# Loading the experts' weights as 16 KB per partition: a one-core transformer layer with expert choice

## Chip, core and metric

The kernel runs on one core of a Trainium2 chip, in one launch. The metric is device time in microseconds (us), the median of three runs. TensorE (PE) multiplies into PSUM, VectorE (DVE), ScalarE (ACT) and GpSimd (POOL) do the rest, and SyncE (SP) issues the loads, which 16 DMA engines carry from HBM to SBUF.

## What is computed

One encoder layer on x, 512 tokens of 1024 features, in float32. Three mixers (windowed attention, a short gated convolution, a bidirectional gated linear attention, GLA) work on one input projection, their outputs are merged by sigmoid gates, projected and added to the residual. Then comes the mixture of experts: 16 experts each choose their 64 best tokens.

```python
x = layer_norm(DN_ALPHA * x + merged @ w_out[l], ln_mix_g[l], ln_mix_b[l])
ffn = expert_choice_ffn(x, router_w[l], expert_w_gate[l], expert_w_up[l], expert_w_down[l])
x = layer_norm(DN_ALPHA * x + ffn, ln_ffn_g[l], ln_ffn_b[l])
# in expert_choice_ffn, for the 64 tokens xs of each expert:
h = jax.nn.silu(einsum('becd,edf->becf', xs, w_gate)) * einsum('becd,edf->becf', xs, w_up)
y = einsum('becf,efd->becd', h, w_down) * gate[..., None]
```

Each expert has three matrices of 8 MB (gate and up 1024 x 2048, down 2048 x 1024), 24 MB; all 16 have 403 million bytes. Everything else that is loaded is 43 million bytes.

## The kernel before

**Buffers.** Most of SBUF is one pool of 23 slots of 8 KB per partition (`S`, line 40). Every large tile of the whole program takes a slot and gives it back after its last reader. A load or a write into a slot that is not free waits for that reader.

**The front** (lines 75 to 755) splits the weights and x into high and low parts and computes the projections block by block; the GLA and attention steps are woven between the blocks. The loop of line 836 computes gates, branches and merge in 24 units, each with a load of 768 KB (`wmr`) that is split (`wmh`, `wml`). While it ends, the raw output weights (`wor`), the rows x (`xres`) and three loads of expert 0 are issued. The output projection runs as two passes (`pw`, `pw2`); the first adds to `xres` at line 924. In and behind the second pass lie the first norm and the router (lines 1032 to 1132): transposes of `xres` (`route_t`, line 938), the logits (`route_m`), the top tokens (`top64`), and the norm's scales and shifts spread over the partitions (`bcast`, line 1091).

**The experts** (lines 1287 to 1373) go in order e = 0 to 15, each gate (`g`), up (`u`) and down (`d`) in eight steps k. `gather` (line 1152) picks the tokens of a pair of experts with a one-hot matrix: in expert 0 for the first pair, in every odd expert for the next pair, one d-tile a step. `ff_mm` multiplies 64 tokens with 128 rows of the matrix, `down` with 256 rows; between them h is transposed (line 1368), and y is combined into the rows two experts later (`combine`). The last expert's down is done by blocks of 256 columns (`last_down`), then the second norm and the stores.

**The order of the loads** is the order of `seq` (line 798): one load of 1 MB per k. SP issues them in this order and stands at the first whose slot is not free.

```python
seq.append((eg[e, k * 128:(k + 1) * 128, :], e, "g", k))
seq.append((ed[e].rearrange("(h q p) d -> q p h d", h=2, p=128)[k], e, "d", k))
```

So a gate or up load brings each partition one row of 8 KB, a down load two rows of 4 KB, and a load of the last expert's down eight pieces of 1 KB. Three loads go out in the merge, 22 in all are queued behind the projection's first pass, 36 after the router, and the rest when the slots for `late`, `acc0` and `acc1` have been taken at the start of e0u (line 1317), where small POOL copies hold the order. Two spare buffers outside the pool take a load each (`early`, `hbt`).

Of the kernel before, what the change touches and what calls it, by code (L numbers as in the profile page):

```python
# [15 lines left out]
NE = 16  # L16
NSLOT = 23
# [4 lines left out]
HB, YB, NPRE, EARLY = 7, 15, 22, 3  # L22
# [6 lines left out]
def tile_hybrid_layer(ctx, tc, pk, w2p, xT, x, wlv, wa, wak, wmb, wout, eg, eu, ed, out):  # L29
# [4 lines left out]
    cpool = ctx.enter_context(tc.tile_pool(name="consts", bufs=1))  # L34
    spool = ctx.enter_context(tc.tile_pool(name="slots", bufs=NSLOT))
# [4 lines left out]
    def S(name, shape, dt=F32):  # L40
        n = 1
        for d in shape[1:]:
            n *= d
        assert n <= 2048
        t = spool.tile([128, 2048], dt, name=name, tag="s")
        v = t[:, :n]
# [4 lines left out]
        return v  # L51

# [22 lines left out]
    # ------------------------------------------------------------ first loads  # L75
    xr = [S(f"xr{i}", [128, 4, 512]) for i in range(2)]
    xh = [S(f"xh{i}", [128, 4, 512], F32R) for i in range(2)]
    xl = [S(f"xl{i}", [128, 4, 512], F32R) for i in range(2)]
    wr = [S(f"wlvr{i}", [128, 3, 672]) for i in range(3)]
    wh = [S(f"wlvh{i}", [128, 3, 672], F32R) for i in range(3)]  # L80
    wl = [S(f"wlvl{i}", [128, 3, 672], F32R) for i in range(3)]
# [9 lines left out]
    # the tensor engine's clock and the activation table are up before the first loads arrive  # L91
    v_sb = S("v_sb", [128, 4, 512])
# [13 lines left out]
    # ------------------------------------------------------------ constants  # L106
# [4 lines left out]
    at_t = S("at_t", [128, 2048])  # L111
# [20 lines left out]
    # ------------------------------------------------------------ GLA low rank, GLA v, attention v  # L132
    misc = S("misc", [128, 4, 512])          # low rank part, attention v, second key tile's decays
    av = misc[:, 1, :].rearrange("p (a b) -> p a b", a=4)
    # the low rank part is stacked three times on the partitions: high, low, high with high, high, low of its weights
# [8 lines left out]
    def b_mm(pb, k):  # L144
        """products of k-tile k, those first whose parts are there first"""
# [42 lines left out]
    raw = {}  # L188
    last_split = {}
# [4 lines left out]
    def load_unit(u, after):  # L194
        if u < 24:
            raw2[u] = S(f"wmr{u}", [128, 12, 128])
            load(raw2[u], wmb[u], after)

    def split_unit(u):
        if u >= 24:  # L200
            return
        h = S(f"wmh{u}", [128, 12, 128], F32R)
        l = S(f"wml{u}", [128, 12, 128], F32R)
        w2[u] = (h, l)
        A.copy(h, raw2[u])  # L205

        def low():
            sp2[u] = V.tensor_sub(l, raw2[u], f32(h))  # L208
            load_unit(u + 2, sp2[u])
        later.append(low)  # L210

    def load_chunk(c):
# [4 lines left out]
        raw[c] = S(f"wr{c}", [128, 2 if two else 1, 1024])  # L217
# [8 lines left out]
    def split_block(n, now=False):  # L226
# [4 lines left out]
        t = S(f"wb{n}", [128, 2, 1024], F32R)  # L231
# [28 lines left out]
    # ------------------------------------------------------------ GLA  # L260
    gqk = S("gqk", [128, 2, 2, 512])             # [q|k, tile, t]
    adec = {}                                    # (direction, tile) -> decay [128, 512]
# [48 lines left out]
    def ytile(b):  # L311
        y[b]["h"] = S(f"y{b}h", [128, 4, 512], F32R)
        y[b]["l"] = S(f"y{b}l", [128, 4, 512], F32R)
# [5 lines left out]

    class Gla:  # L320
        """one pass over the two heads of key tile i"""
# [8 lines left out]
        def start(self):  # L330
            i = self.i
            if i == 0:
                self.ps = S("gps0", [128, 4, 512])
# [3 lines left out]
            else:  # L337
                self.ps = S("gps1", [128, 2, 512])
# [5 lines left out]
        def prep(self, m):  # L344
            """factors of level m (blocks of 2m tokens, decays to the middle)"""
# [14 lines left out]
            if "qk2" not in st:  # L360
                st["qk2"] = S("qk2", [128, 2, 2, 512])
# [43 lines left out]
        def post(self, m):  # L405
            if m >= 256:
                # the rows of k and the state of each half of the tokens
# [8 lines left out]
            if m == 0:  # L416
                a = S(f"gA{self.i}", [128, 4, 512])
# [80 lines left out]
    def weave(a, b):  # L498
        """the steps of two lists in turn, so that neither waits for its own last step"""
# [7 lines left out]
    # ------------------------------------------------------------ attention  # L507
    aq = [S(f"aq{i}", [128, 4, 512], F32R) for i in range(2)]     # high and low parts
    ak = S("ak", [128, 2, 512], F32R)
# [9 lines left out]
    class Att:  # L519
        """heads j and j + 4, query block b"""  # L520
# [7 lines left out]
        def scores(self):  # L528
            j, b = self.j, self.b
            self.ps = [P("ps0"), P("ps1")]  # L530
            for g in range(2):
                hp = slice(g * 64, g * 64 + 64)
                for n, (lq, lk) in enumerate(((0, 0), (0, 1), (1, 0))):
                    PE.matmul(self.ps[g][:, :self.n], aq[lq][hp, j, b * 128:(b + 1) * 128],
                              ak[hp, lk, self.s0 * 128:self.s1 * 128], start=n == 0, stop=n == 2)
# [64 lines left out]
    # ------------------------------------------------------------ short convolution  # L600
# [25 lines left out]
    # ------------------------------------------------------------ side work beside the blocks  # L626
# [3 lines left out]
    class Step:  # L630
        """work beside a segment of the blocks: before it, on the tensor engine after it, and afterwards"""
# [38 lines left out]
    def overlay(a, b, at):  # L670
        """steps b beside steps a from position at of a"""
# [17 lines left out]
    def main_evac(nm, p):  # L689
# [5 lines left out]
        elif kind == "aq":  # L695
            h, l = (t[:, int(nm[2]), :] for t in aq)
            A.activation(h, p, AF.Copy, scale=0.125)
            later.append(lambda: V.scalar_tensor_tensor(l, p, 0.125, f32(h), op0=OP.mult, op1=OP.subtract))
        elif kind == "ak":
            A.copy(ak[:, 0, :], p)  # L700
            later.append(lambda: V.tensor_sub(ak[:, 1, :], p, f32(ak[:, 0, :])))
        elif kind == "gr":
            h = int(nm[2])
            if h == 0:
                st["rs"] = S("rsil", [128, 4, 512])
# [51 lines left out]
    # ------------------------------------------------------------ gates, branches, merge  # L757
    order = ("g", "c", "a")
    accs, mh, ml = [], [], []
    # ------------------------------------------------------------ output projection: its weights  # L760
# [6 lines left out]
    def load_wo(half, after):  # L767
        for c in range(2):
            wraw[half, c] = S(f"wor{half}{c}", [128, 4, 512])
# [3 lines left out]
    def load_rest(after):  # L773
        for i in range(2):
            xres.append(S(f"xres{i}", [128, 2, 1024]))
            load(xres[i], x[i * 256:(i + 1) * 256, :].rearrange("(a p) d -> p a d", p=128), after)
        load_wo(1, None)

    def wo_tiles(half, c):
        woh[half, c] = S(f"woh{half}{c}", [128, 4, 512], F32R)  # L780
        wol[half, c] = S(f"wol{half}{c}", [128, 4, 512], F32R)

    def wo_split(half, k):
        c = k // 4
        if (half, c) not in woh:
            wo_tiles(half, c)
# [10 lines left out]
    # ------------------------------------------------------------ expert weights  # L797
    seq = []
    for e in range(NE):
        for k in range(8):  # L800
            seq.append((eg[e, k * 128:(k + 1) * 128, :], e, "g", k))
        for k in range(8):
            seq.append((eu[e, k * 128:(k + 1) * 128, :], e, "u", k))
        for k in range(8):
            if e < NE - 1:
                seq.append((ed[e].rearrange("(h q p) d -> q p h d", h=2, p=128)[k], e, "d", k))
            else:
                src = ed[e].rearrange("(f p) d -> p f d", p=128)
                seq.append((src[:, k % 2 * 8:k % 2 * 8 + 8, k // 2 * 256:k // 2 * 256 + 256], e, "d", k))
    # the spare buffers take a load each: y's an early one, h's the last one before the experts begin  # L810
    seq = (seq[:EARLY] + [seq[YB]] + seq[EARLY:HB] + seq[HB + 1:YB] + seq[YB + 1:NPRE + 1] + [seq[HB]]
           + seq[NPRE + 1:])
    chunk = {}
    nload = [0]

    def load_experts(upto, after):
        while nload[0] < min(upto, len(seq)):
            src, e, kind, k = seq[nload[0]]
            if nload[0] == EARLY:
                t = st["spare"].tile([128, 2048], F32, name="early")  # L820
            elif nload[0] == NPRE:
                t = st["hbt"]
            else:
                t = S(f"e{e}{kind}{k}", [128, 2048])
            if kind == "d":
                t = t.rearrange("p (a b) -> p a b", a=src.shape[1])
            if nload[0] == len(seq) - 1:
                for f0, f1 in ((0, 4), (4, 6), (6, 8)):
                    load(t[:, f0:f1], src[:, f0:f1])
            else:  # L830
                load(t, src, after)
            after = None
            chunk[e, kind, k] = t
# [663 lines left out]
```

## Time and profile before

| what | value |
|---|---|
| three runs, device time | 1485.08, 1485.46, 1487.37 us (median 1485.46) |
| profiled execution: span of its core, its own time | 1485.3 us |
| mean granted TensorE clock | 0.989 |
| busy: PE, DVE, ACT, POOL | 1380.5, 447.0, 288.3, 88.9 us |
| DMA | 449.32 MB in 89631 packets, mean 303 GB/s |
| packets under 8 KB | 55248 |
| chain that ended last | PE 65%, DMA 27%, DVE 6% |

Busy time is a mean over stages with different limits: PE is busy for 93% of the span, yet 27% of the chain of work that ended last is DMA. The chain is followed back from the last instruction, at each step to what released it. GB/s is what all 16 DMA engines moved; a packet is one contiguous piece of a transfer.

### The profile page before, as it was taken

The page shows a single profiled execution, that of the slowest core. Times are in us where ns is not written, and L with a number is a line of the kernel's source. Part 1 is how long each engine was busy: PE and PEld are TensorE (multiplying, and loading weights), DVE is VectorE, ACT ScalarE, POOL GpSimd, SP SyncE. Part 2 cuts the span into 40 slices and gives each one's busy share as a digit, 9 for nine tenths or more (in the row PEclk, how much of TensorE's full clock was granted, in tenths as well). Part 3 has the DMA queues.
Part 4 walks back from the last instruction along what each step waited for, and adds up shares of the span by engine and source line. Part 5 has one row for each costly group of instructions (what it writes and reads, how often), then busy time and mean ns, then how long its engine had stood idle before and what let it go on. Part 6 is the DMA issues. An engine that isn't in the chain of part 4 may idle for free.

```text
span 1485.3 us, 17870 instructions
## 1 busy us (share of the span) xinstructions
PE 1380.5 (93%) x7458; PEld 770.7 (52%) x7458; DVE 447.0 (30%) x903; ACT 288.3 (19%) x546; POOL 88.9 (6%) x127
## 2 busy tenths in 40 slices
PE   9988999999999989999999889989979989998995
PEld 8765777888888855533434423422523433332343
DVE  5569586423344533112021011002011011000236
ACT  4623455222234120101001000100100100000011
POOL 0267200000000010000000000000000000000001
PEclk9999999999999999999999999999999999999998
DMA  6110121232338689999999999999999999999995
GB/s 224 44 58 34 53 69 60 85 107 85 107 129 339 276 338 383 398 415 421 414 417 419 414 421 415 415 420 415 419 416 415 421 414 418 418 415 420 415 384 169
DMA packets 89631, 449.32 MB, mean 303 GB/s; under 512 B 7280, under 2 KB 15600, under 8 KB 55248
## 3 DMA queue, kind: packets, MB, share of 16 engines
q1 hardware_dynamic: 89552, 448.20, 75.5%
q8 instruction: 58, 0.95, 0.3%
q14 instruction: 21, 0.17, 0.0%
HBM read 446.07 MB, written 2.10 MB: 302 GB/s over the span
## 4 chain that ended last, share of the span: by engine, by line
PE 65%; DMA 27%; DVE 6%; issue 1%; ACT 0%; POOL 0%; SPq 0%; DVEq 0%; POOLq 0%; ACTq 0%
PE pgt L1208 10%; PE pup L1208 10%; PE py L1216 5%; PE pxg L1156 5%; PE pm L858 3%; PE pm L860 3%; PE pm L859 3%; PE pa L248 3%; PE pa L250 2%; PE pa L249 2%; PE pb L150 2%; PE pbr L868 1%; PE pbr L867 1%; PE pbr L866 1%; DMA e5d<-in_ed_dram 1%; DMA e14g<-in_eg_dram 1%
## 5 line engine op out<-in xcount | busy, mean ns | idle before, releaser
L1201 DVE TENSOR_TENSOR acc<-acc,pcb 128x512 f32<-128x512 f32 x64 | 41.1, 684 | 221.5 <-PE pcb L1199 221.5
L1225 DVE SCALAR_TENSOR_TENSOR yl<-py,small,late 64x512 fp32r<-64x512 f32 x30 | 22.5, 749 | 246.3 <-ACT late L1224 246.3
L1156 PEld LDWEIGHTS pxg<-Sg,xres 128*128 128x128 f32 x512 | 61.9, 191 | 50.6 <-issue 43.0
L248 PE MATMUL pa<-xh,wb 128*128 128x512 f32 x200 | 84.0, 420 | 0.0
L249 PE MATMUL pa<-xl,wb 128*128 128x512 f32 x200 | 79.8, 399 | 0.0
L250 PE MATMUL pa<-xh,wb 128*128 128x512 f32 x200 | 79.7, 399 | 0.0
L858 PE MATMUL pm<-xh,wmh 128*128 128x512 f32 x192 | 74.8, 390 | 0.0
L859 PE MATMUL pm<-xl,wmh 128*128 128x512 f32 x192 | 74.7, 389 | 0.0
L860 PE MATMUL pm<-xh,wml 128*128 128x512 f32 x192 | 74.7, 389 | 0.0
L1156 PE MATMUL pxg<-Sg,xres 128*128 128x128 f32 x512 | 73.8, 287 | 0.1
L1224 ACT ACTIVATE late<-py,small 64x512 fp32r<-64x512 f32 x30 | 20.5, 682 | 265.8 <-PE py L1216 253.7
L1370 ACT COPY hbt<-pht 128x512 f32<-128x512 f32 x16 | 9.4, 585 | 250.1 <-PE pht L1368 250.1
L1364 DVE TENSOR_TENSOR hbt<-pup,hbt 128x512 f32<-128x512 f32 x32 | 22.1, 692 | 112.2 <-PE pup L1208 112.2
L1150 DVE COPY small<-pgt 128x2 f32<-128x2 f32 x8 | 1.3, 159 | 172.1 <-PE pgt L1148 172.1
L1380 POOL TENSOR_SCALAR small<-small 128x1 f32<-128x1 f32 x1 | 0.2, 227 | 878.0 <-DVE small L1377 878.0
L248 PEld LDWEIGHTS pa<-xh,wb 128*128 128x128 f32 x200 | 38.1, 190 | 11.5 <-issue 2.9
L1359 ACT ACTIVATE hbt<-pgt 128x512 f32<-128x512 f32 x32 | 19.0, 597 | 127.9 <-PE pgt L1208 127.9
L208 DVE TENSOR_TENSOR wml<-wmr,wmh 128x1536 fp32r<-128x1536 f32 x24 | 42.1, 1752 | 4.1 <-ACT wmh L205 4.1
L250 PEld LDWEIGHTS pa<-xh,wb 128*128 128x128 f32 x200 | 38.5, 192 | 8.7
L249 PEld LDWEIGHTS pa<-xl,wb 128*128 128x128 f32 x200 | 38.3, 192 | 6.7
L858 PEld LDWEIGHTS pm<-xh,wmh 128*128 128x128 f32 x192 | 36.0, 188 | 7.7 <-issue 0.2
L859 PEld LDWEIGHTS pm<-xl,wmh 128*128 128x128 f32 x192 | 36.0, 188 | 7.5
(413 smaller groups left out, 2411.3 us busy)
## 6 DMA issues: line engine op xcount, KB each, us to landing
wmr<-in_wmb_dram SPq DMA_DIRECT2D x24, 768.0 KB, 4.2
wr<-in_wa_dram SPq DMA_DIRECT2D x12, 1024.0 KB, 4.8
e0d<-in_ed_dram SPq DMA_DIRECT2D x8, 1024.0 KB, 10.7
e1g<-in_eg_dram SPq DMA_DIRECT2D x8, 1024.0 KB, 4.8
e1u<-in_eu_dram SPq DMA_DIRECT2D x8, 1024.0 KB, 7.2
e1d<-in_ed_dram SPq DMA_DIRECT2D x8, 1024.0 KB, 7.9
e2g<-in_eg_dram SPq DMA_DIRECT2D x8, 1024.0 KB, 6.3
e2u<-in_eu_dram SPq DMA_DIRECT2D x8, 1024.0 KB, 10.4
```

The source lines that it names most:

```text
L150: PE.matmul(p[:, :336], a, w, start=k == 0 and part == 0, stop=k == 7 and part == 2)
L208: sp2[u] = V.tensor_sub(l, raw2[u], f32(h))
L248: PE.matmul(p, w[:, 0, k, :], XH(k), start=k == 0, stop=False)
L249: PE.matmul(p, w[:, 0, k, :], XL(k), start=False, stop=False)
L250: PE.matmul(p, w[:, 1, k, :], XH(k), start=False, stop=k == 7)
L858: PE.matmul(p, h[:, k, :], XH(k), start=k == 0, stop=False)
L859: PE.matmul(p, h[:, k, :], XL(k), start=False, stop=False)
L860: PE.matmul(p, l[:, k, :], XH(k), start=False, stop=k == 7)
L1156: PE.matmul(p[:, 0:128], xr_(tb)[:, d * 128:(d + 1) * 128], Sg[:, tb].rearrange("p a b -> p (a b)"), start=tb == 0, stop=tb == 3)
L1201: V.tensor_add(r, r, p)
L1208: PE.matmul(p[c][g * 64:(g + 1) * 64, :], l, w[:, g * 1024 + c * 512:g * 1024 + c * 512 + 512], start=k == 0, stop=k == 7)
L1216: PE.matmul(p[g * 64:(g + 1) * 64, :], hT[:, k, half * 64:(half + 1) * 64], w[:, half, dh * 512:(dh + 1) * 512], start=k == 0 and half == ...
```

## The change

The pool of 23 slots becomes ten buffers of 16 KB (`D`) and five of 8 KB (`S`). A `D` holds one expert load of 2 MB, for which rows of the matrices are dealt to the partitions anew: partition p takes the 2 (gate, up) or 4 (down) adjacent rows 2p, 2p + 1 (4p to 4p + 3), 16 KB in one piece. The rows of k-tile k are then every second row of 256, so the gather, the router's transposes, the scales and shifts use every second column (`every2`), and the transposes of h every fourth; the last expert's down keeps its blocks of 256 columns, two of the old loads to a buffer.

In the front, tiles that live at the same time share a `D`: the raw, high and low parts of x's and the first weights' pieces, `v_sb` with `gqk`, `at_t` with `misc`, `gps0` with `gA0`, `rsil` with `gA1`, `qk2` with `gps1`, each branch's high and low part, each unit's `wmh` with `wml`, the two halves of every part of the output weights. Raw loads and split blocks get fixed places (`raws`, `wbs`) in place of rotating slots. Two pairs are loaded early in place of three loads, and x's rows after them; the second half of e0's gate comes as four 8 KB halves; the load into `hbt` and the POOL copies go.

```diff
-NSLOT = 23
-HB, YB, NPRE, EARLY = 7, 15, 22, 3
+NPAIR, NSLOT = 10, 5
+EARLY = 2
...
+    def D(name, *shapes, dt=F32):
+        t = dpool.tile([128, 4096], dt, name=name, tag="d")
+        out, at = [], 0
...
+            out.append(shaped(t[:, at:at + n], shape))
+            at += n
...
-        h = S(f"wmh{u}", [128, 12, 128], F32R)
-        l = S(f"wml{u}", [128, 12, 128], F32R)
+        h, l = D(f"wm{u}", [128, 12, 128], [128, 12, 128], dt=F32R)
...
+    def halves(e, kind, j):
+        r, w = (4, ed) if kind == "d" else (2, eg if kind == "g" else eu)
+        return w[e].rearrange("(j p r) f -> j p (r f)", p=128, r=r)[j]
...
+    pairs = [(0, "g", 0), (0, "g", 1)] + [(e, kind, j) for e in range(NE) for kind in "gud" for j in range(4)
+                                          if (e, kind) != (0, "g")]
+    npair = [0]
+
+    def load_pairs(upto):
+        for e, kind, j in pairs[npair[0]:upto]:
+            t = chunk[e, kind, j] = D(f"e{e}{kind}{j}", [128, 4096])[0]
+            if kind != "d" or e < NE - 1:
+                load(t, halves(e, kind, j))
+                continue
+            t = chunk[e, kind, j] = t.rearrange("p (f d) -> p f d", f=16)
+            src = ed[e].rearrange("(f p) d -> p f d", p=128)[:, :, j * 256:(j + 1) * 256]
+            cuts = (0, 8, 16) if j < 3 else (0, 8, 12, 14, 16)
+            for f0, f1 in zip(cuts, cuts[1:]):
+                load(t[:, f0:f1], src[:, f0:f1])
+        npair[0] = max(npair[0], upto)
+
+    def load_halves(j, tiles):
+        for r, t in enumerate(tiles):
+            load(t, halves(0, "g", j)[:, r * 2048:(r + 1) * 2048])
+        chunk[0, "g", j] = tiles
...
-            load_rest(None)
-            load_experts(EARLY, None)
+            load_wo(1, None)
+            load_pairs(EARLY)
+            load_x()
...
-    load_experts(NPRE, pin)
+    load_halves(2, [S(f"e0g2{r}", [128, 2048]) for r in range(2)])
+    load_halves(3, [S("e0g30", [128, 2048]), spare.tile([128, 2048], F32, name="e0g31")])
+    load_pairs(NPAIR)
...
+    def every2(d):
+        c = d // 2 * 256 + d % 2
+        return slice(c, c + 255, 2)
...
-            PE.transpose(p[:, k * 128:(k + 1) * 128], xr_(tb)[:, c:c + 128], ident)
+            PE.transpose(p[:, k * 128:(k + 1) * 128], xr_(tb)[:, every2(half * 4 + k)], ident)
...
-            PE.matmul(p[:, k * 128:(k + 1) * 128], ones, d, start=True, stop=True)
+            PE.matmul(p[:, every2(k) if i < 2 else slice(k * 128, (k + 1) * 128)], ones, d, start=True, stop=True)
...
-            PE.matmul(p[:, 0:128], xr_(tb)[:, d * 128:(d + 1) * 128], Sg[:, tb].rearrange("p a b -> p (a b)"),
+            PE.matmul(p[:, 0:128], xr_(tb)[:, every2(d)], Sg[:, tb].rearrange("p a b -> p (a b)"),
...
-                    for t, upto in ((late[:, 0, 0:1], 40), (acc[0][:, 0, 0:1], 44), (acc[1][:, 0, 0:1], len(seq))):
-                        load_experts(upto, G.tensor_copy(t, one[:, 0:1]))
+                    load_pairs(len(pairs))
...
+                        c0, step = (c * 512 + i, 4) if e < LAST else (c * 512 + i * 128, 1)
+                        PE.transpose(p[:, i * 128:(i + 1) * 128], hb[:, c0:c0 + 127 * step + 1:step], ident)
...
-    nc = _bacc.Bacc("TRN2", target_bir_lowering=False, num_devices=1)
+    nc = _bacc.Bacc("TRN2", target_bir_lowering=False, num_devices=1, dynamic_dma_scratch_size=256)
```

## Rows read from the trace of the kernel before

**Rows 1.** Page, 40 slices of the span: DMA busy in tenths, GB/s; packet sizes.
```profile
DMA  6110121232338689999999999999999999999995
GB/s 224 44 58 34 53 69 60 85 107 85 107 129 339 276 338 383 398 415 421 414 417 419 414 421 415 415 420 415 419 416 415 421 414 418 418 415 420 415 384 169
DMA packets 89631, 449.32 MB, mean 303 GB/s; under 512 B 7280, under 2 KB 15600, under 8 KB 55248
```

**Rows 2.** Stage table: stretch, length, busy us (instructions) of each engine, clock, DMA, GB/s.
```profile
core 0: us, PE busy (x) PEld busy (x) DVE busy (x) ACT busy (x) POOL busy (x), PEclk, DMA share, GB/s
533.00:822.00 289.00, 287.89 (x1503) 128.17 (x1504) 44.30 (x84) 34.86 (x64) 0.67 (x3) 1.00 0.99 401
822.00:1402.00 580.00, 518.03 (x2524) 196.16 (x2522) 69.61 (x133) 49.55 (x89) 0.00 (x0) 1.00 1.02 417
```

**Rows 3.** Chain of waits in order of time, after 822 us: start, length, what.
```profile
822.59 20.92 DMA e5d<-in_ed_dram
...
1383.57 18.22 DMA e15g<-in_eg_dram
1401.83 1.94 PE pgt L1208 x8
```

**Rows 4.** DMA summaries of two stretches, 974 to 1009 and 1014 to 1030 us.
```profile
DMA packets 2023, 14.74 MB, mean 421 GB/s; under 512 B 225, under 2 KB 225, under 8 KB 225
...
DMA packets 1691, 6.54 MB, mean 409 GB/s; under 512 B 97, under 2 KB 97, under 8 KB 1690
```

**Rows 5.** Stage table, a later stretch of up loads and one of down loads.
```profile
1338.00:1371.00 33.00, 27.14 (x125) 8.02 (x126) 2.39 (x6) 3.63 (x6) 0.00 (x0) 1.00 1.01 421
...
1379.00:1391.00 12.00, 11.79 (x58) 4.20 (x52) 4.16 (x9) 0.58 (x1) 0.00 (x0) 1.00 1.03 410
```

**Rows 6.** Tile e8g, issue to landing; waits of SP's queue (us, times, longest).
```profile
DMA to landing us min/median/max: 18.2/19.9/20.1
...
SPq L63 <- DMA e8g<-in_eg_dram: 16.8, 8, 2.1
```

**Rows 7.** Chain of waits in order of time, expert 0 to expert 5.
```profile
538.23 1.87 PE pgt L1208 x8
540.10 1.09 PE pxg L1156 x8
...
544.14 1.87 PE pgt L1208 x8
...
556.59 13.76 PE pup L1208 x64
...
586.97 3.45 PE pgt L1208 x16
...
796.13 3.43 PE pgt L1208 x16
```

**Rows 8.** Timeline of SP's issues from 435 to 560 us: first issue, length, count.
```profile
445.96 2.90 SPq L63 DMA_DIRECT2D xres<-in_x_dram  x2
...
510.31 7.05 SPq L63 DMA_DIRECT2D e0d<-in_ed_dram  x7
...
540.14 18.54 SPq L63 DMA_DIRECT2D e1g<-in_eg_dram  x7
```

**Rows 9.** Page, DMA issues: count, KB each, median us from issue to landing.
```profile
wmr<-in_wmb_dram SPq DMA_DIRECT2D x24, 768.0 KB, 4.2
```

**Rows 10.** Timelines of PE and DVE: first matmul of the projection, first use of x.
```profile
464.85 0.39 PE L793 MATMUL pw<-woh,mh 128*128 128x512 f32 x1
...
484.77 0.69 DVE L924 SCALAR_TENSOR_TENSOR xres<-xres,pw 128x512 f32<-128x512 f32 x1 [7.17 <-PE pw L795]
```

**Rows 11.** Weight loads by line and shape: count, busy us, mean ns, idle before.
```profile
L1156 PEld LDWEIGHTS pxg<-Sg,xres 128*128 128x128 f32 x512 | 61.9, 191 | 50.6 <-issue 43.0 <-ACT hbt L1359 4.9 <-DVE Sg L1139 1.7
...
L1208 PEld LDWEIGHTS pup<-e3u,xgb 128*64 128x64 f32 x64 | 7.4, 137 | 4.8 <-issue 1.1
```

**Rows 12.** Timeline from 508 to 535 us: the broadcasts on POOL and PE.
```profile
524.16 6.07 POOL L1098 TENSOR_SCALAR Sg<-ident,pk 128x128 f32<-128x128 f32 x16 [3.04 <-DVE xga L1002]
...
524.59 6.18 PE L1102 MATMUL pbc<-Sg,one 128*128 128x128 f32 x32 [1.95 <-POOL Sg L1098]
```

More of the change, by code (lines that the diff above doesn't have):

```diff
@@ L34, in tile_hybrid_layer @@
     cpool = ctx.enter_context(tc.tile_pool(name="consts", bufs=1))
+    dpool = ctx.enter_context(tc.tile_pool(name="pairs", bufs=NPAIR))
     spool = ctx.enter_context(tc.tile_pool(name="slots", bufs=NSLOT))
@@ L51, in S @@
         return v
+    def D(name, *shapes, dt=F32):
+        t = dpool.tile([128, 4096], dt, name=name, tag="d")
+        out, at = [], 0
+        for shape in shapes:
+            n = 1
+            for d in shape[1:]:
+                n *= d
+            out.append(shaped(t[:, at:at + n], shape))
+            at += n
+        assert at <= 4096
+        return out
     def P(name):
@@ L73, in split @@
         return V.tensor_sub(lo, src, f32(hi))
-    xr = [S(f"xr{i}", [128, 4, 512]) for i in range(2)]
+    Q = [128, 4, 512]
+    xr = D("xr", Q, Q)
     xh = [S(f"xh{i}", [128, 4, 512], F32R) for i in range(2)]
     xl = [S(f"xl{i}", [128, 4, 512], F32R) for i in range(2)]
-    wr = [S(f"wlvr{i}", [128, 3, 672]) for i in range(3)]
-    wh = [S(f"wlvh{i}", [128, 3, 672], F32R) for i in range(3)]
-    wl = [S(f"wlvl{i}", [128, 3, 672], F32R) for i in range(3)]
+    Q3 = [128, 3, 672]
+    wr = D("wlvr", Q3, Q3) + [S("wlvr2", Q3)]
+    wh, wl = (D(f"wlv{c}", Q3, Q3, dt=F32R) for c in "hl")
+    for t, v in zip((wh, wl), D("wlv2", Q3, Q3, dt=F32R)):
+        t.append(v)
     pkt = C("pk", [128, PK_N])
@@ L188, in tile_hybrid_layer @@
     raw = {}
+    raws = D("wr", [128, 2048], [128, 2048])
+    wbs = [D(f"wb{i}", [128, 2, 1024], [128, 2, 1024], dt=F32R) for i in range(2)]
     last_split = {}
@@ L216, in load_chunk @@
         two = c != 4
-        raw[c] = S(f"wr{c}", [128, 2 if two else 1, 1024])
+        raw[c] = shaped(raws[c % 2], [128, 2, 1024])[:, :2 if two else 1]
         load(raw[c], chunk_src[c], last_split.get(c - 2))
@@ L505, in run @@
             f()
-    aq = [S(f"aq{i}", [128, 4, 512], F32R) for i in range(2)]
-    ak = S("ak", [128, 2, 512], F32R)
+    aq = []
     def make_bias(j):
@@ L534, in scores @@
                     PE.matmul(self.ps[g][:, :self.n], aq[lq][hp, j, b * 128:(b + 1) * 128],
-                              ak[hp, lk, self.s0 * 128:self.s1 * 128], start=n == 0, stop=n == 2)
+                              st["ak"][hp, lk, self.s0 * 128:self.s1 * 128], start=n == 0, stop=n == 2)
         def softmax_a(self):
@@ L695, in main_evac @@
         elif kind == "aq":
+            if not aq:
+                aq.extend(D("aq", Q, Q, dt=F32R))
             h, l = (t[:, int(nm[2]), :] for t in aq)
@@ L767, in load_wo, with load_x, wo_tiles @@
     def load_wo(half, after):
-        for c in range(2):
-            wraw[half, c] = S(f"wor{half}{c}", [128, 4, 512])
+        for c, t in enumerate(D(f"wor{half}", Q, Q)):
+            wraw[half, c] = t
             load(wraw[half, c],
                  wout[c * 512:(c + 1) * 512, half * 512:(half + 1) * 512].rearrange("(k p) n -> p k n", p=128), after)
-    def load_rest(after):
+    def load_x():
         for i in range(2):
             xres.append(S(f"xres{i}", [128, 2, 1024]))
[L776 to L781, printed above, removed]
+            load(xres[i], x[i * 256:(i + 1) * 256, :].rearrange("(a p) d -> p a d", p=128))
+    def wo_tiles(half):
+        for nm, t in (("woh", woh), ("wol", wol)):
+            t[half, 0], t[half, 1] = D(f"{nm}{half}", Q, Q, dt=F32R)
     def wo_split(half, k):
         c = k // 4
-        if (half, c) not in woh:
-            wo_tiles(half, c)
+        if (half, 0) not in woh:
+            wo_tiles(half)
         return split(wraw[half, c][:, k % 4, :], woh[half, c][:, k % 4, :], wol[half, c][:, k % 4, :])
@@ L795, in wo_mm @@
         PE.matmul(p, b, woh[half, c][:, kk, :], start=False, stop=k == 7)
[L798 to L809, printed above, removed]
@@ L811, in tile_hybrid_layer @@
-    seq = (seq[:EARLY] + [seq[YB]] + seq[EARLY:HB] + seq[HB + 1:YB] + seq[YB + 1:NPRE + 1] + [seq[HB]]
-           + seq[NPRE + 1:])
-    chunk = {}
[L814 to L833, printed above, removed]
-            nload[0] += 1
+    def halves(e, kind, j):
+        r, w = (4, ed) if kind == "d" else (2, eg if kind == "g" else eu)
+        return w[e].rearrange("(j p r) f -> j p (r f)", p=128, r=r)[j]
@@ L836, in tile_hybrid_layer, with part @@
+    def load_halves(j, tiles):
+        for r, t in enumerate(tiles):
+            load(t, halves(0, "g", j)[:, r * 2048:(r + 1) * 2048])
+        chunk[0, "g", j] = tiles
+    def part(e, kind, k):
+        t = chunk[e, kind, k // 2]
+        return t[k % 2] if isinstance(t, list) else t[:, k % 2 * 2048:k % 2 * 2048 + 2048]
     for u in range(24):
@@ L914, in tile_hybrid_layer @@
     spare = tc.alloc_tile_pool(name="spare", bufs=1)
-    st["hbt"], st["spare"] = hbt, spare
     G.memset(one[:, 0:1], 1.0)
@@ L1003, in top64 @@
         return ops
-    for half, c in ((0, 1), (1, 0), (1, 1)):
-        wo_tiles(half, c)
-        for t in (woh[half, c], wol[half, c]):
-            pin = G.tensor_copy(t[:, 0, 0:1], one[:, 0:1])
     pw = [P(f"pw{tb}") for tb in range(4)]
@@ L1203, in ff_mm @@
     def ff_mm(p, e, kind, k):
-        w = chunk[e, kind, k]
+        w = part(e, kind, k)
         l = XG[(e // 2) % 2][:, k, (e % 2) * 64:(e % 2) * 64 + 64]
@@ L1211, in down @@
     def down(p, e, k):
-        w = chunk[e, "d", k]
-        for half in range(2):
+        w = part(e, "d", k)
+        half = k // 4
+        for r in range(2):
             for g in range(2):
                 dh = g ^ (e % 2)
-                PE.matmul(p[g * 64:(g + 1) * 64, :], hT[:, k, half * 64:(half + 1) * 64],
-                          w[:, half, dh * 512:(dh + 1) * 512], start=k == 0 and half == 0,
-                          stop=k == 7 and half == 1)
+                PE.matmul(p[g * 64:(g + 1) * 64, :], hT[:, k % 4 * 2 + r, half * 64:(half + 1) * 64],
+                          w[:, r * 1024 + dh * 512:r * 1024 + dh * 512 + 512], start=k == 0 and r == 0,
+                          stop=k == 7 and r == 1)
     def y_out(p, e):
@@ L1236, in last_down @@
     def last_down(k):
-        w, b = chunk[LAST, "d", k], k // 2
+        b = k // 2
+        w = chunk[LAST, "d", b][:, k % 2 * 8:k % 2 * 8 + 8]
         if k % 2 == 0:
```

49 lines of the change are left out of this document (22 added, 27 removed).

## The prediction

> **What bounds the kernel now.** I read the time slices first, then the table of stages, the waits in order of time, and the DMA summaries of single stretches. In the slices the 16 DMA engines are at 9 tenths from about 590 us to the end, at 414 to 421 GB/s; before that they are mostly idle [rows 1]. The stage table splits the experts in two: from 533 to 822 us TensorE has 1 us of gaps, from 822 to 1402 us it is idle for 62 of 580 us while DMA moves 417 GB/s [rows 2]. The chain of waits says the same: after 822 us it runs through pieces of about 20 us that are the experts' loads in flight; the last is e15g, whose first load lets TensorE begin at 1401.83 us. From there the chain is TensorE and VectorE alone, 1485.3 - 1401.8 = 83.5 us [rows 3]. So the end is the landing of e15g's first load plus 83.5 us; the landing is set by when the stream begins to run without pauses, by its bytes and by its rate.
>
> The rate follows the length of a contiguous row. In the stretch from 974 to 1009 us only gate and up loads flow: 2023 packets, 225 of them under 512 B (the completion writes), none other under 8 KB, 421 GB/s. From 1014 to 1030 us only down loads flow, whose partition gets two pieces of 4 KB, at 409 GB/s [rows 4]. I looked at 12 stretches of the first kind (420 to 422) and 15 of the second (408 to 411); one more of each stands in [rows 5]. Eight loads of 1 MB are in flight at a time: one lands 19.9 us after its issue, eight times 2.49 us, and SyncE's queue waits for landings before it issues again [rows 6]. The queue is never short, and this limit counts loads, not bytes.
>
> **The change, part by part.** The profiled span, 1485.3 us, stands 0.2 us under the median of the three runs, 1485.46 us; the sum is made against the span.
>
> *Packets.* At 421 GB/s an engine takes 8192 x 16 / 421 = 311.3 ns for an 8 KB packet, at 409 GB/s 160.2 ns for one of 4 KB [rows 4]. Two of the latter cost 9.1 ns more than one of the former, so a packet costs 9.1 ns beside its bytes. One of 16 KB then takes 2 x 311.3 - 9.1 = 613.5 ns: 427 GB/s. No row shows a 16 KB load. Bounds: no better than 8 KB, 421; no packet cost left at all, 4096 bytes in 160.2 - 9.1 ns, 434. I take 427, the straight line through both kinds of row. Before, an expert's 24 loads of 1 MB take 16 x 2.49 + 8 x 2.56 = 60.4 us, or 5.030 us per 2 MB; after, 2 MB take 4.908 us (bounds 4.835 and 4.981).
>
> [...]
>
> *When the stream begins to run.* The first ten pairs and four 8 KB halves are all of expert 0, so the first load of expert 1 needs the buffer of pair 0, free when k = 1 of e0g is through, at 538.23 + 1.87 = 540.1 us; pair 1 is free at 546.0 us [rows 7]. Before, e1g's first load was issued at 540.14 us by the same release [rows 8]. The rest of e0g lies in 8 KB slots, which go to late, acc0 and acc1, so DMA pauses until e0u frees a pair: 556.59 + 13.76 / 4 = 560.0 us [rows 7]. From there a pair is freed each 3.4 us and takes 4.9 us to load, so loads queue up and DMA runs through. In e1g the gathers slow the releases to 5.9 us (544.14 - 538.23), but by then some five are waiting. Pairs 10 and 11 are in by 552 us; pair 12 flows from 560.0 us, with 2.3 us once for start and landing (768 KB landed in 4.2 us, of which 1.9 us are bytes at 421 [rows 9]).
>
> *Sum.* e15g's first pair is number 2 + 8 + 14 x 12 = 178, so 167 pairs from number 12 on: 560.0 + 2.3 + 167 x 4.908 = 1381.9 us, plus 83.5 gives 1465.4 us. With the rate of before the same sum gives 560.0 + 2.3 + 167 x 5.030 + 83.5 = 1485.8 us, within 0.5 us of what was measured. So the new buffers alone are worth nothing, and the rate 167 x 0.122 = 20.4 us. That e15g now waits for 2 MB at once is in the pair count.
>
> *The end.* The last expert's down loads keep their 1 KB pieces, their order and a last piece of 256 KB. They flow under the 83.5 us of TensorE's work; behind e15g's first pair come 7 pairs (34.4 us) and 8.4 MB of small pieces, less than before behind its first 1 MB. Cost nothing; cover gone, the wait adds one for one.
>
> *The front.* Paired tiles hold a buffer until both halves are done. At the tightest point, the output projection's first pass, the ten are mh, ml, the raw, high and low parts of both halves of the weights, and two early pairs: all are used, none is missing. What moves is the load of x: it was issued at 445.96 us [rows 8] and now stands behind the second early pair, whose buffer comes free when the merge ends, about 465 us (the projection's first matmul is at 464.85 us). Two megabytes of pair and two of x take 10 us plus 2.3, so x lands near 478 us and is first read at 484.77 us [rows 10]. Six microseconds of cover; cost nothing, and one for one if gone. The down loads of e0, issued from 510.31 us on [rows 8], move to the end of the projection's second pass; they are wanted after e0u, which begins at 556.59 us. The loads into hbt and the POOL copies that pinned slots go: nothing waited long for them. SyncE issues half as many loads: its queue was waiting, so nothing.
>
> *Strided reads.* Weight loads of the gather and of the router's transposes now take every second column, those of h's transposes every fourth. No row shows a stride. A load of 128 columns takes 191 ns, of 64 columns 137 ns [rows 11]: 54 ns per 64 columns, 107 for 128, under a step of 136 ns (8 in 1.09 us [rows 7]). At full rate nothing; at half rate the step is 214 ns, 0.078 us more. Ahead of e1g there are 32 + 64 + 8 such steps, 8.1 us, which delay the releases; later ones lie under DMA. I take 1 us, near the low end, because weight loads have 29 ns of cover in the step. The writes of the broadcasts with a step of two cost nothing while POOL, at 6.07 us for 16, sets their pace [rows 12].
>
> [...]
>
> Sum: 1465.4 + 1 + 0.2 = 1466.6, say 1466 us.
>
> **The rivals.**
> *A. Long rows run no faster than 8 KB ones*, because a 16 KB row is moved as two packets or the path is full at 421. For it: no slice exceeds 421 [rows 1]. Against: the packet cost is visible between 4 and 8 KB. Then 167 x 4.981 = 831.8, and the end is 1478.8 us. [...]
> *B. The start slips* (half-rate weight loads, or x late): 8 to 12 us, 1474 to 1478 us, still faster.
> *C. Slower: strided weight loads make TensorE the bound.* It needs 587.0 to 796.1 us for four experts, 52.3 each [rows 7]. From e1g to e15g it does 14 experts with 560 strided steps, 104 before: with x us more per step the end is 587.0 + 731.9 + 83.5 + 664 x = 1402.4 + 664 x. It decides from x = 0.11, and is slower than before from x = 0.125, near twice the step of now; at a third of the column rate (x = 0.185) it gives 1525 us. For it: a stride was never run here. Against: 29 ns of cover, and only a loss of more than half the rate suffices.
>
> **How the numbers follow.** Forecast 0.60, A 0.16, B 0.10, C 0.09, and 0.05 for an end within 3 us of before (A and B together). A measurement of this kernel tells 0.2% from no change, 3 us. Faster 0.86, same 0.05, slower 0.09. The range goes from 1457 us (packet cost nearly gone: 1454 is the bound) to 1481 us (A with the 1 us, and most of B); it leaves out C.
>
> **What would show it.** Right: stretches of pure 16 KB flow at 425 to 429 GB/s, the landing of e15g's first pair near 1382 us, a pause of DMA between 552 and 560 us, the chain's DMA pieces at two experts per 118 us. Half the packets over 8 KB, none at 4 KB, in the DMA summary. Wrong: 421 in these stretches (A); gather steps over 0.2 us and TensorE without gaps after 900 us (C); VectorE waiting for x's load near 485 us (B).

## The result and the profile after

The changed kernel takes 1471.89 us (median of four runs, 1470.79 to 1471.96); the kernel before, run beside it, 1486.3 us (median of four runs, 1485.08 to 1487.37). The ratio is 0.9901, 95% interval 0.9887 to 0.9915: 14.4 us faster. The forecast was 1466 us, with a range of 1457 to 1481. The profiled execution took 1470.79 us, of which its span is 1469.0. It is the shortest of the four runs, by 1.0 us, so the spans of the two profiles differ by more than the medians, 16.3 us.

The page of the changed kernel, the 40 slices of the span and the packet sizes, against [rows 1]:

```profile
DMA  6111111232237787999999999999999999999994
GB/s 227 44 59 33 54 62 69 86 103 91 95 104 303 322 328 323 427 428 428 427 427 428 428 428 428 428 427 427 427 427 429 428 428 428 428 427 427 427 381 144
DMA packets 47484, 449.28 MB, mean 306 GB/s; under 512 B 4304, under 2 KB 12624, under 8 KB 21552
```

The same bytes come in about half the packets. From the seventeenth slice to the last expert the rate no longer moves between 414 and 421: it stands at 427 to 429.

The table of stages of the changed kernel (stretch, length, busy us of each engine, clock, DMA share, GB/s), against [rows 2, 4]:

```profile
552.00:562.00 10.00, 10.00 (x50) 3.68 (x50) 0.00 (x0) 2.83 (x4) 0.00 (x0) 1.00 0.16 36
562.00:640.00 78.00, 77.75 (x434) 40.46 (x432) 17.23 (x30) 7.40 (x14) 0.00 (x0) 1.00 1.01 428
974.00:1009.00 35.00, 30.17 (x140) 10.37 (x138) 4.17 (x8) 2.27 (x4) 0.00 (x0) 1.00 1.01 428
640.00:1385.70 745.70, 692.27 (x3434) 283.13 (x3430) 96.27 (x184) 71.07 (x128) 0.00 (x0) 1.00 1.01 428
1385.70:1469.00 83.30, 63.89 (x388) 30.86 (x388) 36.81 (x77) 13.38 (x24) 7.32 (x6) 0.91 0.75 282
```

DMA pauses from 552 to 562 us (552 to 560 forecast), and from then on it flows at 428 GB/s until the last expert. TensorE is still idle for 53 of the 746 us behind 640: it is still the loads that it waits for. The next fence is the same view of the kernel before, for the stretch behind the pause:

```profile
562.00:640.00 78.00, 77.51 (x436) 39.65 (x434) 17.33 (x30) 7.39 (x14) 0.67 (x3) 1.00 0.99 398
```

Before, there was no such pause (347 GB/s from 552 to 562 us), but the stream ran at 398 GB/s in this stretch. Few loads were in flight: one of 1 MB landed 6.3 to 10.4 us after its issue (medians of e1u to e2u; 19.9 us later on [rows 6]), and in slices of 2 us the rate fell to 210 GB/s near 576 us and to 324 near 616 us. SyncE's queue waited for TensorE's releases for 65.6 of the 78 us. The old stream thus started in another way than the new one; this matters below.

The chain of waits of the changed kernel in order of time (start, length, what), against [rows 3, 7]:

```profile
532.56 2.06 PE pxg L1171 x16
...
556.24 13.76 PE pup L1223 x64
...
839.02 39.16 DMA e6u<-in_eu_dram
...
1193.39 39.92 DMA e12u<-in_eu_dram
...
1346.27 39.41 DMA e15g<-in_eg_dram
1385.72 1.94 PE pgt L1223 x8
```

A load of 2 MB is under way for 39.1 us (issue to landing of tile e8g); at 428 GB/s that is eight loads of 2 MB in flight, as it was eight of 1 MB before [rows 6]. The end is built as before: the last expert starts when its first pair has landed, at 1385.7 us against 1401.8, and 1469.0 - 1385.7 = 83.3 us follow (83.5 before). So nearly the whole gain of the two profiles lies ahead of this landing: 16.1 of 16.3 us.

### The profile page after: what moved, and what is told of

Its sections match the earlier page's. It is cut to its first block, busy times and chain, and to the rows that moved or that the text cites. A ratio compares the mean times of both kernels' runs of the same rounds, so it can differ in the third digit from the quotient of the medians.

```text
span 1469.0 us, 17474 instructions
## 1 busy us (share of the span) xinstructions
PE 1374.3 (94%) x7458; PEld 785.2 (53%) x7458; DVE 447.0 (30%) x903; ACT 288.3 (20%) x546; POOL 87.7 (6%) x118
## 4 chain that ended last, share of the span: by engine, by line
PE 52%; DMA 40%; DVE 6%; ACT 0%; issue 0%; POOL 0%; SPq 0%; DVEq 0%; ACTq 0%; POOLq 0%
PE pgt L1223 7%; PE pup L1223 6%; PE py L1232 4%; PE pm L874 3%; PE pm L876 3%; PE pm L875 3%; DMA e12u<-in_eu_dram 3%; DMA e8u<-in_eu_dram 3%; DMA e5g<-in_eg_dram 3%; DMA e7g<-in_eg_dram 3%; DMA e11g<-in_eg_dram 3%; DMA e15g<-in_eg_dram 3%; DMA e13g<-in_eg_dram 3%; DMA e9g<-in_eg_dram 3%; DMA e9d<-in_ed_dram 3%; DMA e6u<-in_eu_dram 3%
## 5 line engine op out<-in xcount | busy, mean ns | idle before, releaser
L1171 PEld LDWEIGHTS pxg<-Sg,xres 128*128 128x128 f32 x512 | 65.1, 196 | 50.5 <-issue 43.1
L1171 PE MATMUL pxg<-Sg,xres 128*128 128x128 f32 x512 | 77.1, 294 | 0.0
L874 PE MATMUL pm<-xh,wm 128*128 128x512 f32 x192 | 74.8, 390 | 0.0
L875 PE MATMUL pm<-xl,wm 128*128 128x512 f32 x192 | 74.7, 389 | 0.0
L876 PE MATMUL pm<-xh,wm 128*128 128x512 f32 x192 | 74.7, 389 | 0.0
L227 DVE TENSOR_TENSOR wm<-wr,wm 128x1536 fp32r<-128x1536 f32 x24 | 42.0, 1751 | 4.1 <-ACT wm L224 4.1
L874 PEld LDWEIGHTS pm<-xh,wm 128*128 128x128 f32 x192 | 36.0, 188 | 7.6 <-issue 0.2
L876 PEld LDWEIGHTS pm<-xh,wm 128*128 128x128 f32 x192 | 36.0, 188 | 7.5
```

The lines of the kernel that those rows point to most:

```text
L874: PE.matmul(p, h[:, k, :], XH(k), start=k == 0, stop=False)
L875: PE.matmul(p, h[:, k, :], XL(k), start=False, stop=False)
L876: PE.matmul(p, l[:, k, :], XH(k), start=False, stop=k == 7)
L1171: PE.matmul(p[:, 0:128], xr_(tb)[:, every2(d)], Sg[:, tb].rearrange("p a b -> p (a b)"), start=tb == 0, stop=tb == 3)
```

## The experiments

**1. The row's length alone.** Two kernels halve each 2 MB load. Both keep the buffers, the order, the strided reads and 1 MB per load; one has rows of 8 KB, the other rows of 16 KB in every other partition. A third splits the partitions into lower and upper 64.

```diff
-                load(t, halves(e, kind, j))
+                for r in range(2):
+                    c = slice(r * 2048, (r + 1) * 2048)
+                    load(t[:, c], halves(e, kind, j)[:, c])
```

> The changed kernel (16 KB buffers, their order and the strided reads kept), with each 2 MB load of the experts taken as two loads of 1 MB whose rows are 8 KB. Theory (the row's length makes the gain): packets of about 309 to 311 ns, 420 to 422 GB/s in every stretch of gate, up and down loads, 4.98 us per 2 MB against 4.91, over 167 pairs 12 us more than the changed kernel: 1483 to 1485 us, or 1.5 us less, since the last expert's first tile then waits for 1 MB alone. Rival (buffers, order and the number of loads make the gain): within 2 us of the changed kernel's 1472 us.

```diff
-                load(t, halves(e, kind, j))
+                for pp in (slice(0, 64), slice(64, 128)):
+                    load(t[pp], halves(e, kind, j)[pp])
```

> The changed kernel with each 2 MB load taken as two loads of 1 MB that have 64 partitions each, so that the rows stay at 16 KB while the load is halved and 8 MB instead of 16 MB are in flight. Theory (only the row's length sets the rate): 427 to 428 GB/s as in the changed kernel, 1470 to 1473 us, landings of about 20 us. Rival (it is the size of a load, or 16 MB in flight, that makes the rate): 421 GB/s and about 1483 us.

```diff
-                load(t, halves(e, kind, j))
+                for s in range(2):
+                    load(t[s::2], halves(e, kind, j)[s::2])
```

> The changed kernel with each 2 MB load taken as two loads of 1 MB again, rows of 16 KB, but now one load has the even partitions and the other the odd ones, not the lower and the upper 64. Theory (only the row's length sets the rate; a load into 64 neighbouring partitions is slow because it writes to half of the buffer memory's range at a time): packets of 613 ns, 427 to 428 GB/s, 1470 to 1473 us. Rival one (it is the size of a load, or 16 MB in flight, that makes the rate of the changed kernel): 421 GB/s, 1483 us. Rival two (any load of 64 partitions is slow): packets near 1200 ns and some 2060 us, as with the lower and upper halves.

Measured: 1481.76 us with rows of 8 KB (five runs, 1481.52 to 1482.0; ratio to the kernel before, run beside it, 0.9969, interval 0.9957 to 0.9981), 1470.9 us with rows of 16 KB in every other partition (four runs, 1470.81 to 1471.35; 0.9899, 0.9886 to 0.9913), and 2060.84 to 2219.54 us with the lower and upper halves (six runs; the three shortest, up to 2076.4 us, give a ratio of 1.39). The DMA summary of the first, 974 to 1009 us:

```profile
DMA packets 2025, 14.75 MB, mean 421 GB/s; under 512 B 226, under 2 KB 226, under 8 KB 226
```

Of the kernel with every other partition, the stage table from 640 to 1360 us, then issue to landing of tile e8g:

```profile
640.00:1360.00 720.00, 669.04 (x3334) 282.99 (x3332) 89.97 (x172) 69.75 (x126) 0.00 (x0) 1.00 1.01 428
...
DMA to landing us min/median/max: 19.5/19.5/19.6
```

Rows of 16 KB run at 428 GB/s though a load has 1 MB and only 8 MB are in flight; rows of 8 KB run at 421 with the same load size. So among these kernels it is the row's length that sets the rate, and neither the load's size nor the bytes in flight. Between the two kernels lie 10.9 us. The first starts its last expert on half a pair, though; by the landing of the whole pair (1376.42 + 19.82 from its chain of waits, and 2.5 us for the second half) it is 1398.7 against 1385.7 us, 13 us where 12.2 were forecast.

The lower and upper halves came out by neither theory nor rival (1470 to 1473 and 1483 us): they leave the question asked open and answer another. The stage table and the tile e8g of this kernel (the profile is of its longest run):

```profile
700.00:2100.00 1400.00, 900.64 (x3402) 332.93 (x3398) 93.67 (x177) 69.03 (x125) 0.00 (x0) 0.83 1.00 235
...
DMA to landing us min/median/max: 35.8/35.9/35.9
```

With rows of the same length DMA is busy all the time at 235 GB/s, little over half of 428. In the shortest run it is some 260 GB/s, an estimate: the stream of 1558 us at 235 GB/s, from 562 to 2120 us, shortened by the 159 us between the two runs. Rival two of the expectation, any load of 64 partitions is slow, fell with every other partition. The two kernels differ only in which 64 partitions a load has: 235 against 428 GB/s. The reason that the expectation names, half of the buffer memory's range at a time, agrees with both rates; no view here shows it, and it stays the author's supposition.

**2. New buffers with the rows of before.** The mapping of rows is undone, and with it the strided reads; the 16 KB buffers and their order stay. The down loads become two loads of 1 MB to a buffer (their lines are not shown).

```diff
-        r, w = (4, ed) if kind == "d" else (2, eg if kind == "g" else eu)
-        return w[e].rearrange("(j p r) f -> j p (r f)", p=128, r=r)[j]
+        if kind == "d":
+            return ed[e].rearrange("(h j a p) d -> j p a h d", h=2, a=2, p=128)[j]
+        return (eg if kind == "g" else eu)[e].rearrange("(j a p) f -> j p a f", a=2, p=128)[j]
...
-        c = d // 2 * 256 + d % 2
-        return slice(c, c + 255, 2)
+        return slice(d * 128, (d + 1) * 128)
```

> The changed kernel with its 16 KB buffers and their order, but with the rows as they were before: gate and up loads of 2 MB in pieces of 8 KB, down loads of 1 MB in pieces of 4 KB, and plain columns everywhere. Theory (the row's length makes the gain, the new buffers are worth nothing or a few us of loss): 5.03 us per 2 MB on the mean of an expert, 20 us more than the changed kernel, 1489 to 1492 us, so at or above the kernel before (1486 us); 421 GB/s in gate and up stretches, 409 in down stretches. Rival (the buffers make part of the gain): clearly under 1486 us.

Measured: 1492.16 us (five runs, 1490.57 to 1495.31), ratio 1.0044, 1.0032 to 1.0056: 0.4% slower than the kernel before, just above the 1489 to 1492 us expected. From its chain of waits, its timeline of PE and its stage table:

```profile
1384.67 20.86 DMA e15g<-in_eg_dram
...
1405.57 3.54 PE L1228 MATMUL pgt<-e15g,xgb 128*64 128x512 f32 x8 [3.05 <-DMA e15g<-in_eg_dram]
...
1405.57:1409.04 3.47, 3.47 (x8) 0.77 (x9) 0.00 (x0) 0.00 (x0) 0.00 (x0) 0.53 1.01 423
```

The first pair of the last expert lands at 1405.5 us, 19.8 later than in the changed kernel: that is what the rows are worth (20.4 forecast), less what their strided reads cost. And the new buffers alone cost 6.0 us against the kernel before, by the medians; 5.1 us by the spans (1490.4 and 1485.3). The landing is 3.7 us later than there: 2.5 us would be the second MB that the last expert waits for, at 421 GB/s, and about 1.2 us more are not explained. TensorE then has waited for 3.05 us, and its granted clock is 0.53 in the next 3.5 us (in the stage table of the kernel before it is 0.50 from 522 to 528 us): the first eight matmuls take 3.54 us, where the kernel before had 1.00 and 1.94 us, behind 0.54 us of waiting. So 84.9 us follow the landing instead of 83.5. In this kernel's chain of waits the first 16 matmuls of e5, e7, e9, e11 and e13 take 5.28 to 5.35 us each, where those of e3 take 3.43. The mean granted clock of the five runs is 0.977 to 0.982, of the kernel before 0.989 in its profile: a part of the 6.0 us is the clock, 1.4 us behind the last landing. That longer waits lower it is the author's supposition.

**3. Old buffers with rows of 8 KB in the down loads, and the strides alone.** Both edit the kernel before. The first takes the whole mapping of the change at 8 KB per piece; the second only the step of two, with gate and up rows 16 KB apart, and with the broadcasts written to every second column.

```diff
-            seq.append((eg[e, k * 128:(k + 1) * 128, :], e, "g", k))
+            seq.append((eg[e].rearrange("(j p r) f -> j r p f", p=128, r=2)[k // 2, k % 2], e, "g", k))
...
-                seq.append((ed[e].rearrange("(h q p) d -> q p h d", h=2, p=128)[k], e, "d", k))
+                seq.append((ed[e].rearrange("(j p s r) d -> j s p (r d)", p=128, s=2, r=2)[k // 2, k % 2], e, "d", k))
```

> The kernel before, with its 8 KB buffers and its 1 MB loads, but with the changed kernel's mapping of rows: a partition's piece of a down load is 8 KB instead of twice 4 KB, gate and up pieces stay at 8 KB, and the reads are strided as in the changed kernel. Theory: only the down loads gain, 2 x 0.07 us per 2 MB, 4 x 15 of them: 8.4 us under the kernel before, less about 1 us for the strided reads: 1478 to 1479 us. Rival (rows matter only from 16 KB on, or the gain comes from the buffers): 1486 us. Rival (the strided reads hold up the releases at the start): 1482 us or more, with down stretches at 421 GB/s all the same.

> The kernel before with the strided reads of the gather and of the router's transposes alone (step of two; the gate and up rows of a load lie 16 KB apart to match, in pieces of 8 KB as before; the down loads and the transposes of h are as before). Theory (a step of two costs a weight load 5 ns, under the matmul beside it): 1486 to 1487 us, as the kernel before. Rival (strided reads hold up the first releases, and that is the 2 us by which the down rows of 8 KB alone gained less than expected): 1488 to 1490 us.

(The second kernel has the first changed line, and the same for up, and not the second.) Measured: 1480.8 us for the whole mapping (five runs, 1479.72 to 1481.55; 0.9962, 0.9949 to 0.9975), 1487.96 us for the strides alone (eleven runs, 1486.95 to 1489.02; 1.0012, 1.0003 to 1.0021). Of the whole mapping the DMA summary from 1014 to 1030 us, where only down loads flow, and the timeline of PE:

```profile
DMA packets 924, 6.75 MB, mean 422 GB/s; under 512 B 101, under 2 KB 101, under 8 KB 101
```

```profile
1394.19 1.94 PE L1211 MATMUL pgt<-e15g,xgb 128*64 128x512 f32 x8 [0.55 <-DMA e15g<-in_eg_dram]
```

Two pieces of 4 KB made into one of 8 KB lift the down stretches from 409 to 422 GB/s, in the old buffers. The last expert starts 7.6 us earlier in the profile (8.4 less 1 forecast); the medians differ by 5.4, so the time lies above the 1478 to 1479 us expected and under the second rival's 1482. The strides alone cost 1.9 us by the medians (0.4 to 3.1 by the interval); their profile starts the last expert 0.8 us later than before. That is between theory and rival, and the 1 us that the forecast took lies inside. It does not part the strided reads from the spacing of the rows and the broadcasts. The kernel with the whole mapping and the 8 KB one of experiment 1 have the same rows and load sizes: 1480.8 and 1481.76 us, so with equal loads the old and the new buffers differ by 1 us, less than the intervals tell apart.

**4. The size of the last expert's first load.**

```diff
-                load(t, halves(e, kind, j))
+                cuts = (0, 2048, 4096) if (e, kind, j) in ((NE - 1, "g", 0), (NE - 2, "d", 3)) else (0, 4096)
+                for a, b in zip(cuts, cuts[1:]):
+                    load(t[:, a:b], halves(e, kind, j)[:, a:b])
```

> The changed kernel, with two of its 180 pairs (the last down pair before the last expert, the last expert's first gate pair) loaded in two halves of 1 MB each. Theory (the last expert starts when its first tile has landed, and 3 us of the forecast's error are the size of that load): TensorE begins the last expert 1.4 to 2.4 us earlier, near 1383.5 us instead of 1385.7, and the end comes that much earlier: 1469.5 to 1470.5 us. Rival (the 3 us were lost at the start of the stream alone): 1472 us, as the changed kernel.

Measured: 1471.0 us (four runs, 1470.33 to 1471.57; 0.99, 0.9885 to 0.9916), 0.9 us under the changed kernel by the medians, which the intervals do not tell from nothing (that of the changed kernel is 0.9887 to 0.9915); the spans differ by 0.4 us. Its timeline of PE:

```profile
1383.34 1.94 PE L1225 MATMUL pgt<-e15g,xgb 128*64 128x512 f32 x8 [0.36 <-DMA e15g<-in_eg_dram]
1390.70 3.65 PE L1225 MATMUL pgt<-e15g,xgb 128*64 128x512 f32 x16 [1.19 <-DMA e15g<-in_eg_dram]
1395.60 1.94 PE L1225 MATMUL pgt<-e15g,xgb 128*64 128x512 f32 x8 [0.58 <-DMA e15g<-in_eg_dram]
```

The last expert starts 2.4 us earlier, as the theory said, but then waits 1.19 and 0.58 us for its next pairs. Most of the 2.4 us is given back: behind the first landing there is next to no slack. The time lies between the theory's 1469.5 to 1470.5 us and the rival's 1472. And 2.4 us is half a pair (4.9 / 2), which a smaller first load brings whatever the forecast's error comes from, so this kernel does not say where that error lies.

**5. Less work behind the last landing.**

```diff
+    beside = [(LAST - 2, "d", 4), (LAST - 1, "g", 2), (LAST - 1, "u", 2), (LAST - 1, "d", 2)]
...
+                if e == LAST - 1 and kind == "d" and k == 4:
+                    st_pair()
+                if (e, kind, k) in beside:
+                    c = beside.index((e, kind, k))
+                    A.copy(gb2[:, c // 2, (c % 2) * 512:(c % 2) * 512 + 512], bcast(2 + c // 2, c % 2, dgl))
...
-                        if k == 1:
-                            st_pair()
...
-                        if 2 <= k < 6:
-                            c = k - 2
-                            A.copy(gb2[:, c // 2, (c % 2) * 512:(c % 2) * 512 + 512], bcast(2 + c // 2, c % 2, dgl))
```

> The changed kernel with 8.5 us of TensorE's work that does not depend on the last expert's loads (the four broadcasts of the last norm, the transposed one-hot of the last pair) moved from behind the landing of the last expert's first pair to the two experts ahead of it, where TensorE waits for loads. Theory (the 83.5 us behind that landing have almost no slack to the loads: the last expert's up loads land at 1420 us and its last down piece near 1444 us, 2.6 us ahead of its use): 2 to 3 us of the 8.5 are gained, 1469 to 1470 us, and TensorE waits for e15u and e15d. Rival (the tail is TensorE's work alone, with cover enough): 8 us gained, 1464 us. Rival (the work moved ahead delays the last expert by as much): 1472 us.

Measured: 1469.07 us (four runs, 1468.44 to 1469.94; 0.9886, 0.9873 to 0.99), 2.8 us under the changed kernel by the medians and the lowest of all; no run of the one reaches a run of the other, though the intervals of the ratios overlap. Its timeline of PE:

```profile
1387.26 7.04 PE L1223 MATMUL pgt<-e15g,xgb 128*64 128x512 f32 x32
...
1409.58 3.65 PE L1223 MATMUL pup<-e15u,xgb 128*64 128x512 f32 x16 [0.85 <-DMA e15u<-in_eu_dram]
1414.49 3.65 PE L1223 MATMUL pup<-e15u,xgb 128*64 128x512 f32 x16 [1.25 <-DMA e15u<-in_eu_dram]
1419.41 3.65 PE L1223 MATMUL pup<-e15u,xgb 128*64 128x512 f32 x16 [1.27 <-DMA e15u<-in_eu_dram]
...
1435.30 1.95 PE L1261 MATMUL py<-e15d,hbt 128*64 128x256 f32 x16 [0.98 <-DMA e15d<-in_ed_dram]
```

Of 8.5 us, 1.5 went where the work went (the last expert starts at 1387.3), and 4.4 became waits for e15u and e15d. By this count 2.6 us are left as the gain; the spans differ by 2.3 us, the medians by 2.8.

## Why the prediction was right, and where it was off

**Packets: right.** The forecast took 427 GB/s, and the stretch of 974 to 1009 us shows 428. Experiments 1 and 2 measure the term from two sides, 13 us against rows of 8 KB (12.2 forecast) and 19.8 us against the rows of before (20.4). Sixteen packets of 8 KB per engine became eight, over 167 pairs, so 13 us are 9.7 ns a packet; 9.1 were worked out.

**When the stream begins: right.** The first loads of expert 1 were issued at 539.53, 545.54 and 559.72 us (540.1, 546.0, 560.0 forecast). The timeline of SP's queue, from 530 to 640 us, has the first of them, and the DMA summary of 558 to 562 us the landing of the third:

```profile
539.53 23.94 SPq L79 DMA_DIRECT2D e1g<-in_eg_dram  x4
```

```profile
e1g<-in_eg_dram SPq DMA_DIRECT2D x1, 2048.0 KB, 8.0
```

Pair 12 therefore landed at 559.7 + 8.0 = 567.7 us, 0.5 later than in the sum.

**"after, 2 MB take 4.908 us": the term that was mis-sized.** The count took a pair as landed when so many bytes had flowed at the mean rate. The DMA summary of the changed kernel from 562 to 1385.7 us, the line of the loads' queue:

```profile
q1 hardware_dynamic: 24144, 351.69, 100.4%
```

By the landing, 351.69 MB had been moved, 167.7 pairs of 2.097 MB where the sum has 167. The 0.7 pair belongs to later loads, of which seven are in flight behind the one awaited. From pair 12 to pair 178 a pair takes (1385.7 - 567.7) / 166 = 4.928 us, which is 3.3 us more over the stream. The chain of waits says the same for six experts in its midst: 72 pairs from 878.18 to 1233.31 us, 4.932 each. The trace also keeps 16 landing marks for each load, one for each part of it. Those of pair 12 lie between 566.6 and 567.7 us, those of pair 178 between 1378.9 and 1385.7: the parts drift from 1.1 to 6.8 us apart, and a load counts as landed with its last. The last mark stands 0.8 us behind the mean of its load at pair 12 and 3.3 us at pair 178, which is 2.5 of the 3.3 us. Why the parts drift stays open.

**"So the new buffers alone are worth nothing": wrong.** Experiment 2 puts them at 6.0 us of loss where the rows stay as they were. The forecast's check was that the sum with the rate of before gave 1485.8 us, within 0.5 us of the measured kernel. But the sum modelled the new start (pause, then full flow) and the old kernel starts otherwise (no pause, 398 GB/s until 640 us); the kernel that the sum describes is that of experiment 2, with a span of 1490.4 us. There the same drift costs 4.2 us (by the landing marks of pairs 12 and 178, 566.4 and 1405.5 us, a pair takes 5.055 us and not 5.030), and the slower clock 1.4 us behind the last landing. The agreement was an accident that hid the mis-sized term. In the changed kernel most of that loss is inside the 16.1 us: 20 from the rows, some 4 given back.

**The end: right, with less cover than it looked.** 83.3 us of work follow the landing (83.5 forecast). That chain is TensorE and VectorE, yet experiments 4 and 5 show the loads right behind it: cut the work by 8.5 us and 2.8 are gained.

**The front and the strides: right.** x's two loads were issued from 464.13 us on and took 10.0 and 12.9 us, so they were there at 477.5 (478 forecast) and first read at 483.48 us; nothing waited for them. The weight loads of the gather and of h's transposes, between 562 and 1385 us, against [rows 11]; the third row is of the kernel before, between 562 and 1402 us:

```profile
L1171 PEld LDWEIGHTS pxg<-Sg,xres 128*128 128x128 f32 x448 | 57.0, 196 | 45.5 <-issue 38.2 <-ACT hbt L1375 4.9 <-DVE Sg L1154 2.5
L1386 PEld LDWEIGHTS pht<-ident,hbt 128*128 128x128 f32 x120 | 16.7, 209 | 17.7 <-DVE hbt L1380 17.7
...
L1368 PEld LDWEIGHTS pht<-ident,hbt 128*128 128x128 f32 x120 | 12.6, 141 | 19.8 <-DVE hbt L1364 19.8
```

A step of two takes 196 ns instead of 191, a step of four 209 ns; the kernel before took 141 ns for the latter. The step of two is nearly free here, 5 ns, and the step of four dearer, 68 ns, and that under DMA. Eight gather steps take 1.14 us against 1.09, 0.006 us more a step, so rival C, which needed 0.11, is off by far. The broadcasts, which now write every second column, took 6.52 us (6.18 in [rows 12]); POOL sets their pace here too, with 6.39 us, so what such a write costs by itself is not shown.

**Rivals.** A falls with 428 GB/s in every stretch. B falls with the times of the first issues and of x. The forecast's 5.9 us of error are 0.6 of rounding, 2.6 in the span (3.3 for the pace of pairs and 0.5 for the first landing, less the 1 us for strides, which did not delay the first releases, and 0.2 in the tail), and 2.7 outside it: 1.8 lie around the span of the profiled run and 1.1 between that run and the median, where the forecast had 0.2, because of the kernel before only the span was known.

## What to carry to other kernels

Where a stream of loads bounds a kernel, two kinds of packets in its trace give the cost of a packet, and from it the rate of a longer one; here 427 GB/s were forecast and 428 measured. The bigger loads gained by their rows and not by their size (experiment 1), so put the long row into each partition (428 GB/s with 16 KB, 421 with 8). Where a load has to be cut, cut it over the whole range of partitions, not into a lower and an upper half (428 against 235 GB/s, some 260 in the shortest run by the estimate). Look behind the critical landing before cutting the load that it waits for: here most of the 2.4 us was given back to the loads that came next. Test a formula for the changed kernel on a kernel that it describes: agreement with the old one, which starts otherwise, proves little.

## What the runs showed that was not expected

A load into the lower or the upper 64 partitions ran at 235 GB/s, the same rows into every second partition at 428. A packet's cost beside its bytes is nearly the same from 4 to 16 KB: 9.1 ns between rows of 4 and 8 KB, 9.7 ns between 8 and 16. And the 16 parts of a load fall out of step as the stream runs, in the changed kernel from 1.1 to 6.8 us, in the kernel before from 0.2 us (a load landed at 563 us) to 7.3 us (at 1394 us); a sum of bytes over the mean rate misses that.
